# A hybrid encoder layer: the RWKV chunk step as one 128x128 product, low-rank products over padded rows, identities by ScalarE

## The chip, the cores and the metric

The kernel runs on one core of one Trainium2 chip, in one launch. The time is the device time of that launch in microseconds. Before the change it was 1121.99 us, the median of three runs (1121.66 to 1122.10). A change of 1% is 11 us.

## What is computed

One layer of a streaming encoder on x of shape (1, 512, 1024), all in float32:

```
x = x + 1/2 * SwiGLU_1(RMSNorm(x))
p = RMSNorm(x) @ W_in      -> stick-breaking q | k | v  and  RWKV-7 r | k | v | w-lora | a-lora | g-lora
x = x + concat(stick_breaking_attention(q, k, v), rwkv7(...)) @ W_out
x = x + 1/2 * SwiGLU_2(RMSNorm(x))
```

The RWKV half has 8 heads of 64 channels. Its inputs are shifted by one token; two low-rank maps of 64 columns give the decay and the value a:

```
log_w = -softplus(-(w0 + tanh(x_w) @ w2)) - 0.5      # w2: 64 x 512
a     = sigmoid(a0 + x_a @ a2)                       # a2: 64 x 512
S_t = S_{t-1} diag(w_t) + (S_{t-1} a_t) b_t^T + v_t k_t^T ;  y_t = S_t r_t      # for each head
```

followed by a norm for each head, a bonus term and a gate. The state S (64x64 for each head) starts at zero. The kernel computes the recurrence in 8 chunks of 64 tokens: within a chunk the token loop is turned into the inverse of a 64x64 triangular matrix, and from chunk to chunk one product with a 64x64 matrix M carries the state on.

## The kernel before

Activations lie with channels on the 128 partitions and the 512 tokens along the free dimension. Every float32 matrix product of the dense kind is done as three products of rounded halves (`mm3`, L180 to L183: high by high, high by low, low by high), so each weight tile of 128x512 is loaded by SP (`load`), rounded by ScalarE (ACT, L161) and its rest made by VectorE (DVE, L162). A ring of 3 buffers holds each of the raw, high and low tiles.

There are three stages. The first FFN (to about 366 us of the profiled span) makes 22 blocks of the hidden layer and multiplies them by the down weights (`dn`). Blocks 0 to 3 and every third one after them are plain products; the other twelve come in six pairs, each block done by `seven()` with seven products of half size. Of such a block, `pa`, `pc` and `pe` are PSUM banks; `cu` and `h` are tiles of the ring with tag "a" (4 buffers). The finished `h` is split into `hdh` and `hdl`, which go to rings by the list `home` (L398); blocks 2 to 5 go to the ring with tag "r". `parts` (L279) keeps one pair of tiles of that ring until the last block is done.

The middle stage projects, and runs the attention and the RWKV recurrence for four pairs of heads. The low-rank products stand at its start: `lora` (L543) takes w2 from partitions 0 to 63 and a2 from 64 to 127 of one tile `w2a2`, so each of its products uses 64 rows of the TensorE array. For a pair j, `rw_inverse(j)` builds the chunk matrices and `rw_chain(j)` carries the state. Two heads p = 0, 1 lie on partitions 0 to 63 and 64 to 127 (`rows`), and most small products are done for each head apart, with 64 rows and 64 columns of the array. In `rw_inverse`, A is the product of the two halves AR and BK; A's diagonal blocks go through DRAM (`da`), DVE inverts them by 15 substitution steps (L700 to L704, tiles G and H), they come back through DRAM (`db`), and the products `inv` build the inverse from blocks; Z is an identity tile that GpSimd (POOL) fills (`eye`, L508). Then Q, MG and N give the matrix of the chunk step: after L764 the left half of each chunk in AR holds M, with the identity added that POOL wrote at L695. `rw_chain` makes six steps for c = 1 to 6 (L780): two products S = M St, one for each head, then DVE puts PC*S + St into the next chunk's place (L786).

The attention (`att_core`) makes scores z, an Abs, Exp and Ln on ACT, a scan on DVE (l, r), transposes (wT), an Exp (at) and the output o. Its q and k are normalised by `item_qk`, whose result is called rn (L847).

What sets the order: a Python loop at L954 emits pieces of the dense stream and of the three side queues I (inverse), C (chain) and T (attention) by due times; C and I get a priority (L916). The framework's scheduler then orders each engine's instructions by priority and by its own estimate of when operands and buffers come free, and gives each ring buffer to the next tile once its last reader is done. On each engine the order is fixed in the built program, and each engine works it off in turn.

The last stage is the second FFN, built like the first.

Of the kernel before, what the change touches and what calls it, by code (L numbers as in the profile page):

```python
# [16 lines left out]
F32 = mybir.dt.float32  # L17
# [65 lines left out]
def layer(ctx, tc, a, out, dbg=None):  # L83
# [9 lines left out]
        uid[0] += 1  # L93
        return f"{s}_{uid[0]}"

    NB = {"x": 16, "q": 3, "b": 4, "r": 10, "i": 10, "c": 6, "v": 4, "k": 4, "g": 8, "a": 4, "t": 2, "f": 4, "s": 2, "X": 8}
    NM = {"acc": 2, "sd": 1, "mi": 2, "ma": 3}
    NW = 3
    NPL = 4
# [53 lines left out]
    def load(src, n, s="w"):  # L153
        raw = pw.tile([P, T], F32, tag="raw", name=nm(s), bufs=NW)
        nc.sync.dma_start(raw[:, :n], src)
        return raw

    def w_split(raw, n=T, s="w", pool=nc.vector, cp=nc.scalar.copy):
        hi = pw.tile([P, T], F32R, tag="whi", name=nm(s + "h"), bufs=NW)
        lo = pw.tile([P, T], F32R, tag="wlo", name=nm(s + "l"), bufs=NW)  # L160
        cp(hi[:, :n], raw[:, :n])  # L161
        pool.tensor_tensor(lo[:, :n], raw[:, :n], hi[:, :n].bitcast(F32), SUB)  # L162
        return hi, lo

    def load_split(src, n, s="w", pool=None, cp=nc.scalar.copy):
        if pool is None:
            pool = nc.vector
        return w_split(load(src, n, s), n, s, pool, cp)

    mms = []  # L170
    sp = []
# [191 lines left out]
    def ffn(g, wgu, wd, last):  # L363
# [4 lines left out]
        if last:  # L368
            xsrc = pd.tile([KD, P, T], F32, name="xmid")
            for k in range(KD):  # L370
                nc.sync.dma_start(xsrc[k], X[k])
            xs = norm_in(g, XTAG)
            first = None
        else:
            xs = []

            def first():

                ps = [bank(("acc", "ma")[q], "gu"[q]) for q in range(2)]
                z = slot("f", "warm", BF16)  # L380
                nc.vector.memset(z, 0.0)
                for _ in range(11):
                    nc.tensor.matmul(ps[1], lhsT=z[:, 0:P], rhs=z, start=True, stop=True)
                for k in range(KD):
                    if k:
                        nc.sync.dma_start(X[k], a["xT"][k])
                    if k % 4 == 0:
                        w = [load_split(wgu[q][:, k * P:(k + 4) * P], T, pool=nc.vector,
                                        cp=nc.scalar.copy if k or q else nc.vector.tensor_copy) for q in range(2)]
                    xs.append(split(X[k], XTAG[k], v(g, k), "x"))  # L390
                    ks = slice(k % 4 * P, (k % 4 + 1) * P)
                    for q in range(2):
                        mm3(ps[q], w[q][0][:, ks], w[q][1][:, ks], xs[k][0], xs[k][1], k == 0, k == KD - 1)
                nc.sync.dma_start(cst, a["cst"])
                nc.sync.dma_start(lev, a["lev"])
                return ps
# [90 lines left out]
        return  # L487


    w2a2 = slot("g", "w2a2")  # L490
    nc.sync.dma_start(w2a2, a["w2a2"])
    g2 = slot("f", "g2")
    nc.sync.dma_start(g2, a["g2"])
    seg = slot("r", "seg")
# [12 lines left out]

    def eye():  # L508
        z = slot("i", "Z")
        nc.gpsimd.tensor_scalar(c3(z), cs("i64").unsqueeze(1).to_broadcast([P, NCH, CH]), 1.0, None, MUL)  # L510
        return z

    xs = norm_in("nmx")
# [17 lines left out]
    sgx = slot("f", "sgx")  # L531
    act(sgx, xg, AF.Sigmoid)
    Gs, av = [], []
    wh2 = slot("r", "w2h", F32R)
    nc.scalar.copy(wh2, w2a2)
    wl2 = slot("r", "w2l", F32R)
    nc.gpsimd.tensor_tensor(wl2, w2a2, wh2.bitcast(F32), SUB)
    xh2 = slot("r", "xwh", F32R)
    nc.scalar.copy(xh2, xwa)
    xl2 = slot("r", "xwl", F32R)  # L540
    nc.vector.tensor_tensor(xl2, xwa, xh2.bitcast(F32), SUB)

    def lora(ps, js, rs_):  # L543
        mm3(ps, wh2[rs_, js], wl2[rs_, js], xh2[rs_], xl2[rs_], True, True)

    for j in range(4):
        js = slice(j * P, (j + 1) * P)
        pw_ = bank("sd", "lw")
        lora(pw_, js, slice(0, CH))
        sw = slot("r", "sw")  # L550
        act(sw, pw_, AF.Sigmoid, bias=v("w0", j))
        pa_ = bank("sd", "la")
        lora(pa_, js, slice(CH, P))
        aj = slot("g", "a")
        act(aj, pa_, AF.Sigmoid, bias=v("a0", j))
        gj = slot("g", "Gs")
        nc.vector.tensor_tensor_scan(gj, seg, sw, 0.0, MUL, ADD)
        Gs.append(gj)
        av.append(aj)
# [80 lines left out]
    def rw_inverse(j):  # L640
# [37 lines left out]
            nc.scalar.copy(ba[p][:, :, 0:CH], c3(pt[p]))  # L678
        pta = bank("mi", "tA")
        pw0 = bank("mi", "W0")  # L680
        for c in range(NCH):
            cc = slice(c * CH, (c + 1) * CH)
            for p in range(2):
                nc.tensor.matmul(pta[rows[p], cc], lhsT=ar[rows[p], c, 0:CH], rhs=cs("i64")[rows[p]],
                                 start=True, stop=True)
# [3 lines left out]
                o = rows[1 - p]  # L689
                nc.tensor.matmul(pw0[rows[p], cc], lhsT=Aa[p][o, cc], rhs=UV[p][o, cc], start=True, stop=True)  # L690
        At = slot("i", "At")
        nc.scalar.copy(At, pta)
        W0 = slot("i", "W0")
        nc.scalar.copy(W0, pw0)
        nc.gpsimd.tensor_scalar(ar[:, :, 0:CH], cs("i64").unsqueeze(1).to_broadcast([P, NCH, CH]), 1.0, None, MUL)  # L695
        H = slot("i", "H")
        Xb = c3(H[0:NBK, 0:256], SB)
        nc.gpsimd.memset(H[0:NBK, 0:256], 0.0)
# [24 lines left out]
        Xm, XT = X2  # L723


        def prod(l, r):
            ps = bank("mi", "inv")
            for c in range(NCH):
                cc = slice(c * CH, (c + 1) * CH)
                for p in range(2):  # L730
                    l_ = l[p] if isinstance(l, list) else l
                    nc.tensor.matmul(ps[rows[p], cc], lhsT=l_[rows[p], cc], rhs=r[rows[p], cc], start=True, stop=True)
            return ps
# [12 lines left out]
            nc.scalar.copy(XT, pst)  # L746
            yield 6

        pq, pu = prod(XT, At), prod(XT, W0)
        Q = slot("i", "Q")  # L750
        nc.scalar.copy(Q, pq)
        for p in range(2):
            nc.scalar.copy(UV[p][rows[p]], pu[rows[p]])
        yield 3

        for h in range(2):
            hs = slice(4 * h, 4 * h + 4)
            pm = bank("mi", "MG")
            for c in range(4 * h, 4 * h + 4):
                cp = slice((c % 4) * P, (c % 4 + 1) * P)  # L760
                for p in range(2):
                    nc.tensor.matmul(pm[rows[p], cp], lhsT=Q[rows[p], c * CH:(c + 1) * CH], rhs=ba[p][rows[p], c],
                                     start=True, stop=True)
            nc.vector.tensor_tensor(ar[:, hs], c3(pm, P), ar[:, hs], ADD)  # L764
        pn = bank("mi", "N")
        for c in range(NCH - 1):
            cc = slice(c * CH, (c + 1) * CH)
            for p in range(2):
# [1 line left out]
        St = slot("i", "St")  # L770
        nc.vector.tensor_tensor(c3(St)[:, 1:NCH], c3(pn)[:, 0:NCH - 1],
                                PC[:, 0:NCH - 1].unsqueeze(2).to_broadcast([P, NCH - 1, CH]), MUL)
        ctxs[j].update(ba=ba, ar=ar, St=St)
        yield 3

    def rw_chain(j):

        js = slice(j * P, (j + 1) * P)
        PC, ar, ba, bv, UV, St = (ctxs[j][n] for n in ("PC", "ar", "ba", "bv", "UV", "St"))
        for c in range(1, NCH - 1):  # L780
            cc = slice(c * CH, (c + 1) * CH)
            nn = slice((c + 1) * CH, (c + 2) * CH)
            pS = bank("mi", "S", [P, CH])
            for p in range(2):
                nc.tensor.matmul(pS[rows[p]], lhsT=ar[rows[p], c, 0:CH], rhs=St[rows[p], cc], start=True, stop=True)
            nc.vector.scalar_tensor_tensor(St[:, nn], pS, PC[:, c:c + 1], St[:, nn], MUL, ADD)  # L786
            yield 1.2

        py = bank("mi", "y")
        for c in range(NCH):  # L790
            cc = slice(c * CH, (c + 1) * CH)
            for p in range(2):
                nc.tensor.matmul(py[rows[p], cc], lhsT=UV[p][:, cc], rhs=ba[p][:, c, CH:P], start=c == 0, stop=False)
        for c in range(1, NCH):
            cc = slice(c * CH, (c + 1) * CH)
            for p in range(2):
                nc.tensor.matmul(py[rows[p], cc], lhsT=St[rows[p], cc], rhs=ar[rows[p], c, CH:P],
                                 start=False, stop=c == NCH - 1)

        yc = slot("r", "yc")  # L800
        nc.scalar.copy(yc, py)
        yr = slot("r", "yr")
        act(yr, py, AF.Square)
        pv = bank("mi", "var")
        head_sum(pv, yr)
        act(yr, pv, AF.Ln, scale=1.0 / CH, bias=epsl)
        act(yr, yr, AF.Exp, scale=-0.5)
        nc.vector.scalar_tensor_tensor(yr, yc, v("lnw", j), yr, MUL, MUL)
        nc.vector.scalar_tensor_tensor(yr, yr, v("lnb", j), bv, ADD, ADD)
        pg = bank("mi", "g")  # L810
        nc.tensor.matmul(pg, lhsT=g2[:, js], rhs=sgx, start=True, stop=True)
        o = slot("g", "orw")
        nc.vector.tensor_tensor(o, pg, yr, MUL)
        outs[4 + j] = o
        yield 5
# [174 lines left out]
def host_arrays(inp):  # L990
# [24 lines left out]

    w = i["w_out"].reshape(2, 4, P, 4, 2, P)[::-1]
    d["wo"] = np.ascontiguousarray(w.transpose(1, 3, 2, 4, 0, 5)).reshape(16, P, T)
    d["w2a2"] = np.ascontiguousarray(np.concatenate([i["rw_w2"], i["rw_a2"]], 0))
    d["g2"] = np.ascontiguousarray(i["rw_g2"])
    return d  # L1020

# [18 lines left out]
```

## Time and profile before

| | before |
|---|---|
| median of 3 runs | 1121.99 us |
| profiled execution | 1122.11 us, span 1120.3 us |
| granted TensorE clock, mean | 0.995 |
| TensorE products (PE) busy | 1090.7 us, 97% |
| VectorE (DVE) busy | 727.5 us, 65% |
| ScalarE (ACT) busy | 520.6 us, 46% |
| GpSimd (POOL) busy | 79.3 us, 7% |
| chain that ended last, by engine | PE 78%, DVE 13%, ACT 3% |

The span is the time from the first to the last instruction; the profiled execution took 1.8 us more than its span. A row for a product gives the rows and columns of the array as 128*128, 64*128 (64 rows) or 64*64, then the partitions and elements that move. Float32 products run as two passes, and each pass is a row of its own in the counts; rounded halves (fp32r) run as one. The ends of products are modelled, so the text compares starts. A clock of 1.00 is 2.4 GHz, and the lower level is 1.2 GHz.

### The profile page before, as it was taken

Reading aid. Unit: us, or ns where it says so; the run is one execution under the profiler, and the core shown is the slowest. Engines: PE = TensorE matmul, PEld = TensorE weight load, DVE = VectorE, ACT = ScalarE, POOL = GpSimd, SP = SyncE. Lnnn points to the kernel's source line nnn. Section 1 sums busy time; section 2 is a strip of 40 time slices with the busy share of each in tenths; the row PEclk is TensorE's granted clock in tenths of the full one; section 3 lists DMA queues with packets and bytes.
Section 4 is the critical chain, followed back from the end, with each engine's and each line's share of the span. In section 5 each row is a group of like instructions: output and inputs, shape, how many; then the busy total and the mean of one; then the engine's idle time right before and its main releaser. Section 6 shows DMA issues by size and latency. Waiting matters only on the chain.

```text
span 1120.3 us, 18878 instructions
## 1 busy us (share of the span) xinstructions
PE 1090.7 (97%) x7363; PEld 896.7 (80%) x7363; DVE 727.5 (65%) x1296; ACT 520.6 (46%) x958; POOL 79.3 (7%) x61
## 2 busy tenths in 40 slices
PE   8989999999999999999999998998999999999998
PEld 6789999998888767766667675676889999998886
DVE  6997777763333567577766768587987777753322
ACT  5555545543223564474644554454555545432221
POOL 0100000000003011011100310012100000000000
PEclk9999999999999999999999999999999999999999
DMA  5333333343333224311211211043343333344442
GB/s 193 107 106 95 112 104 114 96 138 101 95 98 94 95 66 140 81 38 50 58 31 50 48 32 39 20 132 124 93 122 101 98 90 109 95 146 113 115 120 62
DMA packets 70697, 104.23 MB, mean 93 GB/s; under 512 B 19664, under 2 KB 21840, under 8 KB 70608
## 3 DMA queue, kind: packets, MB, share of 16 engines
q1 hardware_dynamic: 70608, 103.02, 31.1%
q8 instruction: 58, 0.95, 0.3%
q14 instruction: 31, 0.25, 0.1%
HBM read 97.23 MB, written 5.77 MB: 92 GB/s over the span
## 4 chain that ended last, share of the span: by engine, by line
PE 78%; DVE 13%; ACT 3%; issue 2%; POOL 1%; DMA 1%; SPq 0%; DVEq 0%; ACTq 0%; POOLq 0%
PE dn L183 7%; PE dn L182 7%; PE dn L181 7%; PE pa L181 4%; PE pa L183 4%; PE pa L182 4%; PE g L182 2%; PE g L181 2%; PE g L183 2%; PE pc L183 2%; PE pc L182 2%; PE pc L181 2%; PE u L181 2%; PE u L183 2%; PE u L182 2%
## 5 line engine op out<-in xcount | busy, mean ns | idle before, releaser
L162 DVE TENSOR_TENSOR wl<-w,wh 128x512 fp32r<-128x512 f32 x220 | 151.0, 687 | 200.6 <-ACT wh L161 199.4
L161 ACT CAST wh<-w 128x512 fp32r<-128x512 f32 (+1 forms) x219 | 132.2, 604 | 237.7 <-PE dn L182 153.6
L181 PE MATMUL dn<-hdh,wh 128*128 128x512 f32 x240 | 93.4, 389 | 0.0
L182 PE MATMUL dn<-hdl,wh 128*128 128x512 f32 x240 | 93.4, 389 | 0.0
L183 PE MATMUL dn<-hdh,wl 128*128 128x512 f32 x240 | 93.4, 389 | 0.0
L182 PEld LDWEIGHTS dn<-hdl,wh 128*128 128x128 f32 x240 | 45.1, 188 | 9.3
L181 PEld LDWEIGHTS dn<-hdh,wh 128*128 128x128 f32 x240 | 45.1, 188 | 9.3
L183 PEld LDWEIGHTS dn<-hdh,wl 128*128 128x128 f32 x240 | 45.1, 188 | 9.3
L161 ACT CAST wh<-wg 128x512 fp32r<-128x512 f32 x48 | 29.7, 621 | 38.2 <-PE u L182 21.0
L181 PE MATMUL dn<-hd,wh 128*128 128x512 f32 x112 | 43.6, 389 | 0.0
L182 PE MATMUL dn<-hd,wh 128*128 128x512 f32 x112 | 43.6, 389 | 0.0
L183 PE MATMUL dn<-hd,wl 128*128 128x512 f32 x112 | 43.6, 389 | 0.0
L183 PE MATMUL u<-xnh,wl 128*128 128x512 f32 x96 | 37.5, 390 | 0.9 <-DVE wl L162 0.9
L181 PE MATMUL g<-xnh,wh 128*128 128x512 f32 x96 | 37.6, 391 | 0.0
L182 PE MATMUL g<-xnl,wh 128*128 128x512 f32 x96 | 37.5, 391 | 0.0
L182 PE MATMUL u<-xnl,wh 128*128 128x512 f32 x96 | 37.5, 390 | 0.0
L181 PE MATMUL u<-xnh,wh 128*128 128x512 f32 x96 | 37.5, 390 | 0.0
L183 PE MATMUL g<-xnh,wl 128*128 128x512 f32 x96 | 37.5, 390 | 0.0
L162 DVE TENSOR_TENSOR wl<-wg,wh 128x512 fp32r<-128x512 f32 x48 | 33.0, 686 | 5.5 <-ACT wh L161 5.5
L315 ACT CAST s3h<-s 128x512 fp32r<-128x512 f32 x24 | 14.9, 621 | 41.3 <-DVE s L313 41.3
L181 PE MATMUL pa<-xch,s2h 128*128 128x256 f32 x96 | 27.4, 285 | 3.5 <-ACT cu L332 3.5
L134 ACT ACTIVATE l<-l 128x128 f32<-128x128 f32 (+3 forms) x64 | 28.8, 467 | 0.9
(355 smaller groups left out, 3197.3 us busy)
## 6 DMA issues: line engine op xcount, KB each, us to landing
w<-wgu SPq DMA_DIRECT2D x80, 256.0 KB, 2.9
w<-wd SPq DMA_DIRECT2D x80, 256.0 KB, 2.6
wu<-wgu SPq DMA_DIRECT2D x48, 256.0 KB, 2.9
wg<-wgu SPq DMA_DIRECT2D x48, 256.0 KB, 2.5
w<-wrw SPq DMA_DIRECT2D x28, 256.0 KB, 2.8
x<-xT SPq DMA_DIRECT2D x16, 256.0 KB, 4.8
w<-wqk SPq DMA_DIRECT2D x16, 256.0 KB, 2.7
wv<-wv SPq DMA_DIRECT2D x16, 256.0 KB, 2.6
```

Source lines behind the costliest of these rows:

```text
L134: ins = nc.scalar.activation(out_, in_, func, **kw)
L161: cp(hi[:, :n], raw[:, :n])
L162: pool.tensor_tensor(lo[:, :n], raw[:, :n], hi[:, :n].bitcast(F32), SUB)
L181: mms.append(nc.tensor.matmul(ps, lhsT=lh, rhs=rh, start=start, stop=False, skip_group_check=again))
L182: nc.tensor.matmul(ps, lhsT=lh, rhs=rl, start=False, stop=False, skip_group_check=again)
L183: nc.tensor.matmul(ps, lhsT=ll, rhs=rh, start=False, stop=stop, skip_group_check=again)
L315: nc.scalar.copy(hi, t_)
```

## The change

Four things change.

The chunk step: a new tile `Mb` (ring "m", one buffer) holds for each chunk a 128x128 matrix with head 0's M in the upper left block, head 1's in the lower right, and zero elsewhere. POOL sets it to zero, DVE writes the two blocks from the bank MG with the identity added, and the step is one product with 128 rows and columns. AR keeps only its right half, so POOL's identity in its left half goes, and DVE's addition for AR covers 64 of 128 columns of each chunk. Chunk 0 (whose state before is zero) is left out of tA, of the product with At and of MG.

The low-rank products: `w2a2` becomes two tiles, w2 with zeros below and a2 with zeros above, and each product takes all 128 rows. They need two more tiles of ring "r" and one more load.

Identities: `eye` copies with ACT.

Rings: "r" has 8 buffers instead of 10, which makes room for `Mb`.

```
-    NB = {"x": 16, "q": 3, "b": 4, "r": 10, "i": 10, "c": 6, "v": 4, "k": 4, "g": 8, "a": 4, "t": 2, "f": 4, "s": 2, "X": 8}
+    NB = {"x": 16, "q": 3, "b": 4, "r": 8, "i": 10, "c": 6, "v": 4, "k": 4, "g": 8, "a": 4, "t": 2, "f": 4, "s": 2, "X": 8, "m": 1}
...
-    w2a2 = slot("g", "w2a2")
-    nc.sync.dma_start(w2a2, a["w2a2"])
+    w2a2 = [slot("g", "w2a2") for _ in range(2)]
+    for q in range(2):
+        nc.sync.dma_start(w2a2[q], a["w2a2"][q])
...
     def eye():
         z = slot("i", "Z")
-        nc.gpsimd.tensor_scalar(c3(z), cs("i64").unsqueeze(1).to_broadcast([P, NCH, CH]), 1.0, None, MUL)
+        nc.scalar.copy(c3(z), cs("i64").unsqueeze(1).to_broadcast([P, NCH, CH]))
...
-    def lora(ps, js, rs_):
-        mm3(ps, wh2[rs_, js], wl2[rs_, js], xh2[rs_], xl2[rs_], True, True)
+    def lora(ps, js, q):
+        mm3(ps, w2[q][0][:, js], w2[q][1][:, js], xh2, xl2, True, True)
...
-        for c in range(NCH):
+        for c in range(1, NCH):
...
-        nc.gpsimd.tensor_scalar(ar[:, :, 0:CH], cs("i64").unsqueeze(1).to_broadcast([P, NCH, CH]), 1.0, None, MUL)
+        Mb = quad("Mb", tag="m")
+        mb = c3(Mb, P)
+        nc.gpsimd.memset(Mb, 0.0)
...
-        pq, pu = prod(XT, At), prod(XT, W0)
+        pq, pu = prod(XT, At, 1), prod(XT, W0)
...
         for h in range(2):
-            hs = slice(4 * h, 4 * h + 4)
+            c0 = max(4 * h, 1)
+            hs = slice(c0, 4 * h + 4)
             pm = bank("mi", "MG")
-            for c in range(4 * h, 4 * h + 4):
+            for c in range(c0, 4 * h + 4):
...
-            nc.vector.tensor_tensor(ar[:, hs], c3(pm, P), ar[:, hs], ADD)
+            n = 3
+            for p in range(2):
+                nc.vector.tensor_tensor(mb[rows[p], c0:c0 + n, p * CH:(p + 1) * CH],
+                                        c3(pm, P)[rows[p], c0 % 4:c0 % 4 + n, 0:CH],
+                                        cs("i64")[rows[p]].unsqueeze(1).to_broadcast([CH, n, CH]), ADD)
+            nc.vector.tensor_tensor(ar[:, hs, CH:P], c3(pm, P)[:, c0 % 4:, CH:P], ar[:, hs, CH:P], ADD)
...
-            for p in range(2):
-                nc.tensor.matmul(pS[rows[p]], lhsT=ar[rows[p], c, 0:CH], rhs=St[rows[p], cc], start=True, stop=True)
+            nc.tensor.matmul(pS, lhsT=mb[:, c], rhs=St[:, cc], start=True, stop=True)
```

The host array w2a2 becomes (2, 128, 512) with the zeros in it.

The order of the instructions changes with it, since buffers and products differ. Three places follow. A row names the line, the operation, and its tiles with their buffer numbers; x2 stands for two instructions in a row.

On PE, in the chunk steps of the first pair, before:

```order
L785 MATMUL S_5514<-St_5263,AR_4252 64x64 x2
L183 MATMUL k_5096<-xh_3718,wl_5100 128x512
L181 MATMUL k_5096<-xh_3722,wh_5099 128x512
L182 MATMUL k_5096<-xl_3723,wh_5099 128x512
L785 MATMUL S_5536<-St_5263,AR_4252 64x64 x2
```

and after:

```order
L795 MATMUL S_5517<-St_5268,Mb_4513 128x64
L180 MATMUL k_5101<-xl_3737,wh_5122 128x512
L181 MATMUL k_5101<-xh_3736,wl_5123 128x512
L179 MATMUL k_5101<-xh_3740,wh_5122 128x512
L795 MATMUL S_5538<-St_5268,Mb_4513 128x64
```

Each step is one product over all 128 rows instead of two over 64; the dense products between two steps are as many.

On DVE, at the last pair of heads, the end of the substitution (G and H), with the normalised q and k (rn, of qc) of the last attention item between its steps, before:

```order
L704 TENSOR_REDUCE H_7194<-G_7112 64x12
L809 SCALAR_TENSOR_TENSOR yr_7275<-yr_7275,vec,xv_5304 128x512
L702 TENSOR_TENSOR G_7112<-G_7112,H_7194 64x169
L813 TENSOR_TENSOR orw_7285<-g_7283,yr_7275 128x512
L704 TENSOR_REDUCE H_7194<-G_7112 64x13
L847 SCALAR_TENSOR_TENSOR rn_6298<-qc_6296,derived,rn_6298 128x512
L702 TENSOR_TENSOR G_7112<-G_7112,H_7194 64x196
L847 SCALAR_TENSOR_TENSOR rn_6347<-qc_6345,vec,rn_6347 128x512
```

and after, with the beginning of the same substitution:

```order
L854 TENSOR_TENSOR rn_6345<-qm_6347,S_3829 128x512
L923 TENSOR_TENSOR x_2852<-wo_6808,x_2852 128x512
L857 SCALAR_TENSOR_TENSOR rn_6345<-qc_6343,vec,rn_6345 128x512
L796 SCALAR_TENSOR_TENSOR St_7064<-S_7223,PC_5607,St_7064 128x64
L706 TENSOR_TENSOR G_7102<-G_7102,H_7179 64x1
L708 TENSOR_REDUCE H_7179<-G_7102 64x1
L706 TENSOR_TENSOR G_7102<-G_7102,H_7179 64x4
```

The rn of q and of k have moved from the end of the substitution to a place ahead of its first step.

On ACT, in the first FFN, at a pair of blocks (h_1079 is the older block's result, h_1164 and cu_1163 the newer one's tiles), before:

```order
L134 ACTIVATE cu_1078<-cu_1078 128x512
L337 COPY h_1164<-pc_1161 128x256
L315 CAST s4h_1320<-s_301_1318 128x512
L161 CAST wh_1360<-w_1358 128x512
L193 CAST hd_1258<-h_1079 128x512
L342 COPY cu_1163<-pa_1160 128x256
```

and after:

```order
L134 ACTIVATE cu_1078<-cu_1078 128x512
L313 CAST s4h_1320<-s_301_1318 128x512
L161 CAST wh_1360<-w_1358 128x512
L335 COPY h_1164<-pc_1161 128x256
L191 CAST hd_1258<-h_1079 128x512
L340 COPY cu_1163<-pa_1160 128x256
```

The copy of `pc` has moved behind two casts, and in the built program it now waits for DVE, which must have read the older block's tiles; the split of block 5's result has moved from its place to the end of the block loop.

## Rows read from the trace of the kernel before

**Rows 1.** The page: PE's busy time, and the chain by engine.
```profile
PE 1090.7 (97%) x7363; PEld 896.7 (80%) x7363; DVE 727.5 (65%) x1296; ACT 520.6 (46%) x958; POOL 79.3 (7%) x61
PE 78%; DVE 13%; ACT 3%; issue 2%; POOL 1%; DMA 1%; SPq 0%; DVEq 0%; ACTq 0%; POOLq 0%
```

**Rows 2.** Stages: stretch, length, busy PE PEld DVE ACT POOL, clock, DMA, GB/s.
```profile
380.00:405.00 25.00, 25.00 (x93) 15.76 (x92) 13.29 (x16) 16.88 (x26) 1.35 (x1) 1.00 0.17 53
...
600.00:700.00 100.00, 92.79 (x887) 64.08 (x887) 80.62 (x179) 54.99 (x115) 14.92 (x10) 0.98 0.18 44
```

**Rows 3.** PE in order of time at a chunk step: start, us, instruction.
```profile
515.85 0.40 PE L182 MATMUL k<-xl,wh 128*128 128x512 f32 x1
516.18 0.33 PE L785 MATMUL S<-St,AR 64*64 64x64 f32 x4
516.44 0.50 PE L183 MATMUL k<-xh,wl 128*128 128x512 f32 x1
516.78 0.39 PE L181 MATMUL k<-xh,wh 128*128 128x512 f32 x1
517.01 0.40 PE L182 MATMUL k<-xl,wh 128*128 128x512 f32 x1
```

**Rows 4.** PE in order of time at a low-rank product.
```profile
387.50 0.40 PE L182 MATMUL k<-xl,wh 128*128 128x512 f32 x1
387.83 0.49 PE L181 MATMUL la<-xwh,w2h 64*128 64x512 f32 x1
...
389.06 0.40 PE L181 MATMUL k<-xh,wh 128*128 128x512 f32 x1
```

**Rows 5.** PE in order of time at the norm's sum over partitions.
```profile
371.38 0.39 PE L183 MATMUL wa<-xh,wl 128*128 128x512 f32 x1
371.61 0.95 PE L219 MATMUL ms<-ones,sq 128*128 128x1 f32 x8
372.42 0.49 PE L181 MATMUL xg<-xh,wh 128*128 128x512 f32 x1
```

**Rows 6.** The chain in order of time, 440 to 800: start, us, what.
```profile
463.19 3.26 PE inv L732 x96
...
471.94 1.09 PE MG L762 x16
```

**Rows 7.** Groups by line, 440 to 800: count, busy us, mean ns, idle before.
```profile
L764 DVE TENSOR_TENSOR AR<-MG,AR 128x512 f32<-128x512 f32 x8 | 5.5, 689 | 22.9 <-PE MG L762 22.9
L658 DVE TENSOR_TENSOR Aa<-A,cst 128x256 f32<-128x256 f32 x12 | 4.9, 412 | 2.5 <-PE A L655 2.5
L746 ACT COPY XT<-inv 128x512 f32<-128x512 f32 x8 | 4.7, 586 | 12.1 <-PE inv L732 11.5 <-issue 0.6
```

**Rows 8.** Waits of PE's weight loads, 440 to 800: us, times, longest.
```profile
PEld MG L762 <- DVE AR L764: 1.3, 3, 0.8
```

**Rows 9.** The page's DMA issues: count, KB each, us to landing.
```profile
w<-wrw SPq DMA_DIRECT2D x28, 256.0 KB, 2.8
```

**Rows 10.** PE in order of time at its longest wait, with that wait in brackets.
```profile
678.60 0.49 PE L857 MATMUL z<-rn,rn 64*128 64x128 f32 x4 [3.28 <-DVE rn L847]
...
680.05 0.63 PE L183 MATMUL wo<-orh,wol 128*128 128x512 f32 x1
680.48 0.63 PE L181 MATMUL wo<-osh,woh 128*128 128x512 f32 x1
...
683.47 0.39 PE L181 MATMUL wo<-osh,woh 128*128 128x512 f32 x1
```

**Rows 11.** DVE in order of time before that wait ends.
```profile
677.80 0.75 DVE L847 SCALAR_TENSOR_TENSOR rn<-qc,vec,rn 128x512 f32<-128x512 f32 x1
```

**Rows 12.** DVE, ACT and PE in order of time at a pair of blocks.
```profile
115.14 0.42 DVE L360 TENSOR_TENSOR h<-pa,cu 128x256 f32<-128x256 f32 x1 [0.45 <-PE pa L183]
...
116.58 0.37 ACT L342 COPY cu<-pa 128x256 f32<-128x256 f32 x1 [0.19 <-PE pa L183]
...
117.82 0.28 PE L181 MATMUL pa<-xch,s3h 128*128 128x256 f32 x1
```

More of the change, by code (lines that the diff above doesn't have):

```diff
@@ L156, in load, with w_split @@
         return raw
-    def w_split(raw, n=T, s="w", pool=nc.vector, cp=nc.scalar.copy):
+    def w_split(raw, n=T, s="w", cp=nc.scalar.copy):
         hi = pw.tile([P, T], F32R, tag="whi", name=nm(s + "h"), bufs=NW)
@@ L161, in w_split, with load_split @@
         cp(hi[:, :n], raw[:, :n])
-        pool.tensor_tensor(lo[:, :n], raw[:, :n], hi[:, :n].bitcast(F32), SUB)
+        nc.vector.tensor_tensor(lo[:, :n], raw[:, :n], hi[:, :n].bitcast(F32), SUB)
         return hi, lo
[L165 to L168, printed above, removed]
+    def load_split(src, n, s="w", cp=nc.scalar.copy):
+        return w_split(load(src, n, s), n, s, cp)
     mms = []
@@ L387, in first @@
                     if k % 4 == 0:
-                        w = [load_split(wgu[q][:, k * P:(k + 4) * P], T, pool=nc.vector,
+                        w = [load_split(wgu[q][:, k * P:(k + 4) * P], T,
                                         cp=nc.scalar.copy if k or q else nc.vector.tensor_copy) for q in range(2)]
@@ L533, in layer @@
     Gs, av = [], []
[L534 to L537, printed above, removed]
+    w2 = []
+    for q in range(2):
+        wh2, wl2 = slot("r", "w2h", F32R), slot("r", "w2l", F32R)
+        nc.scalar.copy(wh2, w2a2[q])
+        nc.gpsimd.tensor_tensor(wl2, w2a2[q], wh2.bitcast(F32), SUB)
+        w2.append((wh2, wl2))
     xh2 = slot("r", "xwh", F32R)
@@ L548, in layer @@
         pw_ = bank("sd", "lw")
-        lora(pw_, js, slice(0, CH))
+        lora(pw_, js, 0)
         sw = slot("r", "sw")
@@ L552, in layer @@
         pa_ = bank("sd", "la")
-        lora(pa_, js, slice(CH, P))
+        lora(pa_, js, 1)
         aj = slot("g", "a")
@@ L691, in rw_inverse @@
         At = slot("i", "At")
-        nc.scalar.copy(At, pta)
+        nc.scalar.copy(At[:, CH:], pta[:, CH:])
         W0 = slot("i", "W0")
         nc.scalar.copy(W0, pw0)
-        nc.gpsimd.tensor_scalar(ar[:, :, 0:CH], cs("i64").unsqueeze(1).to_broadcast([P, NCH, CH]), 1.0, None, MUL)
+        Mb = quad("Mb", tag="m")
+        mb = c3(Mb, P)
+        nc.gpsimd.memset(Mb, 0.0)
         H = slot("i", "H")
@@ L723, in rw_inverse, with prod @@
         Xm, XT = X2
-        def prod(l, r):
+        def prod(l, r, c0=0):
             ps = bank("mi", "inv")
-            for c in range(NCH):
+            for c in range(c0, NCH):
                 cc = slice(c * CH, (c + 1) * CH)
@@ L747, in rw_inverse @@
             yield 6
-        pq, pu = prod(XT, At), prod(XT, W0)
+        pq, pu = prod(XT, At, 1), prod(XT, W0)
         Q = slot("i", "Q")
-        nc.scalar.copy(Q, pq)
+        nc.scalar.copy(Q[:, CH:], pq[:, CH:])
         for p in range(2):
@@ L772, in rw_inverse @@
                                 PC[:, 0:NCH - 1].unsqueeze(2).to_broadcast([P, NCH - 1, CH]), MUL)
-        ctxs[j].update(ba=ba, ar=ar, St=St)
+        ctxs[j].update(ba=ba, ar=ar, mb=mb, St=St)
         yield 3
@@ L778, in rw_chain @@
         js = slice(j * P, (j + 1) * P)
-        PC, ar, ba, bv, UV, St = (ctxs[j][n] for n in ("PC", "ar", "ba", "bv", "UV", "St"))
+        PC, ar, mb, ba, bv, UV, St = (ctxs[j][n] for n in ("PC", "ar", "mb", "ba", "bv", "UV", "St"))
         for c in range(1, NCH - 1):
@@ L1017, in host_arrays @@
     d["wo"] = np.ascontiguousarray(w.transpose(1, 3, 2, 4, 0, 5)).reshape(16, P, T)
-    d["w2a2"] = np.ascontiguousarray(np.concatenate([i["rw_w2"], i["rw_a2"]], 0))
+    d["w2a2"] = np.zeros((2, P, T), np.float32)
+    d["w2a2"][0, :CH] = i["rw_w2"]
+    d["w2a2"][1, CH:] = i["rw_a2"]
     d["g2"] = np.ascontiguousarray(i["rw_g2"])
```

## The prediction

> **What bounds the kernel now.** I read the page's busy times and chain first: PE is busy for 97% of the span and carries 78% of the chain that ended last [rows 1]. Then the stage table: through the low-rank products PE has no idle time at all, and in the attention and RWKV stage, at its worst stretch, it still works 92.8 of 100 us, with DVE at 80.6 and ACT at 55 [rows 2]. So a microsecond taken out of PE's stream there is a microsecond of the kernel, unless a wait opens. Then I read PE's instructions in order of time, around the products that change.
>
> In a dense run one 128x512 product starts 0.23 us after the last (516.78 to 517.01). With a chunk step between, 515.85 to 516.78 is 0.93 us where two dense intervals are 0.46: the step costs 0.47 us, though its four passes of 64x64 are tiny [rows 3]. The low-rank product shows why. Its three products of 64 rows cost as much in time as dense ones, yet 387.50 to 389.06 holds five intervals, 1.15 us, and lasts 1.56 [rows 4]. The 0.41 us too many lie at the two places where the array changes from 128 rows to 64 and back; the first shows in the 0.33 from 387.50 to 387.83. That is 0.21 us per change of shape, and for the chunk step 0.41 of its 0.47.
>
> **The change, part by part.** I go through PE's two listings and give each product the rows and columns of the array it uses. Before, the shape changes 241 times, now 179 times. Of the 62 that go, 18 belong to the low-rank products (nine visits, the first being broken in two); the rest are the chunk steps, less what the new order adds elsewhere. At 0.21 that is -13.0 us.
>
> The step itself: its passes now cost 0.47 - 0.41 = 0.06, 24 times 1.4 us. Afterwards a step is two passes with 128 columns of weights and 64 moving columns. No such product is in the trace. The nearest is the norm's sum over partitions, also f32 with 128x128 weights and one moving column: eight passes between two dense products take 371.61 to 372.42, 0.81 us, 0.10 each [rows 5]. From below it is the 0.034 of a 64x64 pass in an unbroken run (3.26 us for 96) [rows 6]; from above a dense product's 0.23. I take 0.10, the row nearest in shape: 0.20 a step, 24 steps 4.8, so +3.4 us net (from 0.2 to 9.6).
>
> Chunk 0 is left out of three sets. In tA and in the product with At, 4 passes of 0.034, 0.14 us, twice for each of four head pairs: -1.1. In MG, 4 passes of 1.09/16 = 0.07, four times: -1.1 [rows 6]. PE in all: -13.0 + 3.4 - 2.2 = -11.8 us, on the path because PE is.
>
> DVE: two 128x512 additions of 0.69 for each pair become six instructions, five of 192 columns and one of 256. A 256-column one takes 0.41 [rows 7]; between the two sizes the slope is 0.0011 us a column, so 192 columns take 0.34 (0.31 if it went by columns alone, 0.41 at most). A pair: 5 x 0.34 + 0.41 = 2.11 against 1.38, four pairs +2.9 us (2.3 to 4.3). Queued behind them are St, whose product starts the chunk chain, and the bank of MG that N wants. Each bank is now held for three instructions, 1.0 us instead of 0.7. Today PE waited for that bank three times, 1.3 us [rows 8]. I put all eight banks at 0.3 on the path: +2.4, out of 0 to 4.3.
>
> The identities: eight copies on ACT at 0.59 [rows 7], 4.7 us, beside PE's work on an engine that is busy for 55 of 100 us; none hangs on data of the step, so I cost them at nothing, 4.7 if that cover is gone. POOL is rid of eight Z and four AR fills and gets a memset of Mb, with H's memset queued behind it; DVE's substitution waits for H, PE does not. The second half of w2a2 is one more 256 KB load on SP (2.8 us to landing [rows 9]), past which the weights of the next products are issued, and one more cast and subtraction; they lie in the stretch where the DMA engines are busy for 17% [rows 2]. Nothing, or up to 2.8.
>
> The order: the scheduler has moved whole items. PE now waits 3.28 us at 675 for the last pair's normalised q and k, and for 3.4 us behind that wait the clock is at its lower level (dense starts 0.43 apart, 680.05 to 680.48): up to 683.47 seven dense products and one transpose take 3.42 us instead of 7 x 0.23 + 0.1 = 1.7 [rows 10]. Cause: DVE makes the last rn at 677.80 only, between the substitution's steps [rows 11]. In the new order both rn stand ahead of that substitution. So -3.3 - 1.7 = -5.0 (from 0, if another such wait comes, to -5.0); I take -4.5, since DVE and ACT have more to do elsewhere.
>
> Sum against the profiled execution's own 1122.11 us (span 1120.3 and 1.8 around it, 0.1 over the median of 1121.99): 1122.1 - 11.8 + 2.4 - 4.5 = 1108.2. **I forecast 1108.2 us.**
>
> A rule that speaks against this: the Trainium skill, TensorEngine Tiling (Array Packing), Theoretical Speedup, has up to 2x for each dimension of 64 or less by splitting the array, so that joining two 64x64 products would give a gain away. By that rule alone the step would only get dearer; the same page (Key Properties) also says that a change of tiling mode drains the engine, and by that the trace agrees with its 0.21 us. The first result is rival 3.
>
> **The rivals.**
> 1. *DVE takes a part back.* For it: 80.6 of 100 us busy, and the stall at 675 was DVE's. If the stall stays in some other place and all 2.9 us of new DVE work end on the path: 1122.1 - 11.8 + 2.9 = 1113.2. Against: the waits of PE for DVE are short elsewhere.
> 2. *All of it comes.* The banks are never waited for and the stall goes whole: 1122.1 - 11.8 - 5.0 = 1105.3.
> 3. *The gaps do not come from the shape but from any small f32 product.* Then no change of shape is won, the step costs 24 x (0.20 - 0.14) = 1.4 more, the fewer products give 2.2, the stall goes: 1122.1 + 1.4 - 2.2 + 2.4 - 4.5 = 1119.2. Against: the low-rank product is not f32-slow and has the gap; the norm's passes are f32 and have none.
> 4. *Slower: the shorter ring.* Ring r has 8 buffers instead of 10, and in both FFNs the hidden tile of block 5 must wait for the end of the block loop to be split, holding one of the four buffers of ring a. So "h<-pc" on ACT now stands behind the old block's last product, with "cu<-pa" two behind it, and PE needs that bank for s3. Place: five pairs in each FFN. Price: today the old product ends on DVE at 115.14 + 0.42, the copy of cu starts at 116.58 and takes 0.37, PE comes at 117.82: 0.87 us of room [rows 12]. The copy in front costs 0.37, so it decides only from half a microsecond of further lateness; 1.9 us too late each would give 1108.2 + 10 x 1.9 = 1127. Against: the cast that stood between has moved ahead of it.
>
> **How the numbers follow.** Forecast 0.55, its own range 1104 to 1112; rival 1 0.17, rival 2 0.13, rival 3 0.06, rival 4 0.07, something else 0.02. The range of 8 in 10 takes in rivals 1 and 2 and the dear end of the step's price (+6.2 over the forecast, 1114) and stops short of 3 and 4: 1102 to 1118. A difference of 0.2% (2.2 us) is about what a measurement here can tell from none. Faster 0.89, the same 0.04 (part of rival 3), slower 0.07.
>
> **What will show it.** Right: between two dense products a chunk step costs 0.2 us instead of 0.47; the low-rank products run at 0.23 with no 0.33 beside them; PE's idle time in the stage does not grow; no 3 us wait and no slow clock near 675. Wrong: steps that still cost 0.4 (rival 3); "issue" time before PE replaced by waits for Mb, St or Z (rival 1); in the FFNs, waits of "pa" for "cu" (rival 4), which would make the time miss by most.

## The result, and the profile after

The changed kernel takes 1109.99 us (median; 1109.11 to 1110.19) where the kernel before took 1122.1 in the same session: a ratio of 0.9887, 95% interval 0.9873 to 0.9902, or 12.1 us less. The forecast was 1108.2 with a range of 1102 to 1118. The time came out 1.8 us from the forecast; the places where it comes from are only partly those that the forecast named.

The profiled execution of the changed kernel took 1110.0 us, its span is 1108.2. Its page answers to [rows 1]; the two stretches and the whole middle stage answer to [rows 2] (stretch, length, busy PE PEld DVE ACT POOL, clock, DMA, GB/s):

```profile
PE 1084.6 (98%) x7267; PEld 898.1 (81%) x7267; DVE 734.8 (66%) x1312; ACT 521.1 (47%) x967; POOL 63.0 (6%) x54
PE 83%; DVE 10%; ACT 3%; issue 2%; DMA 1%; POOL 0%; SPq 0%; DVEq 0%; POOLq 0%; ACTq 0%
```
```profile
372.09:745.65 373.56, 364.26 (x3171) 266.64 (x3170) 277.09 (x553) 204.14 (x391) 29.92 (x30) 0.99 0.22 62
380.00:405.00 25.00, 25.00 (x101) 17.99 (x101) 14.74 (x19) 17.97 (x28) 2.64 (x2) 1.00 0.21 64
600.00:700.00 100.00, 95.52 (x902) 65.67 (x902) 80.27 (x168) 56.07 (x121) 4.68 (x6) 0.97 0.18 43
672.80:679.20 6.40, 6.40 (x17) 4.33 (x17) 4.38 (x12) 2.10 (x6) 0.00 (x0) 0.50 0.00 0
```

The middle stage, from the first product of xg to the first product of the second feed-forward stage, took 384.13 us in the kernel before:

```profile
372.42:756.55 384.13, 371.12 (x3266) 265.71 (x3266) 271.65 (x537) 201.58 (x382) 47.08 (x38) 1.00 0.22 61
```

So 10.6 of the 12.1 us lie in this stage. The rest (0.3 before it, 1.2 behind it) lies in code that is the same in both, but for the order of some instructions; in the experiments below, the time up to the stage varies by -1.7 to +3.1 us, the time from there to the last product by -0.85 to +0.5, whatever the kernel. From here on the stage alone is compared between profiles.

I split its time in three. *Waits* are the bracketed waits in PE's rows in order of time (20 before, 16 after). *Slow clock* is an estimate of what PE loses while the granted clock is 0.50: half of that stretch, since dense starts are 0.43 apart there and 0.23 elsewhere (672.80 to 679.20 above and 0.4 us at its edges make 3.4; before, 1.7). What is left is PE's *own work*. Before: 12.1 + 1.7 + 370.3. After: 8.3 + 3.4 + 361.9. So the own work fell by 8.5 us, waits and slow clock together by 2.1.

The chunk step between two dense products, against [rows 3]:

```profile
513.33 0.39 PE L181 MATMUL k<-xh,wl 128*128 128x512 f32 x1
513.55 0.33 PE L795 MATMUL S<-St,Mb 128*128 128x64 f32 x2
513.69 0.48 PE L179 MATMUL k<-xh,wh 128*128 128x512 f32 x1
514.01 0.39 PE L180 MATMUL k<-xl,wh 128*128 128x512 f32 x1
```

513.33 to 514.01 is 0.68 us, less two dense intervals of 0.23: the step costs 0.22, where 0.20 was forecast, and 0.47 before. It is made of other parts than forecast: the two passes take 0.14 us to the next product's start, not 0.20, and the dense product behind them takes 0.32 instead of 0.23, a gap at full shape for which the forecast had nothing. And three of the 24 steps now stand inside the run of W, a run of 64x64 products. There two 64x64 products had been nearly free, 0.01 us from their start to the next product's, first in the kernel before:

```profile
522.59 0.27 PE L785 MATMUL S<-St,AR 64*64 64x64 f32 x2 [0.27 <-ACT At L692]
522.60 0.27 PE L690 MATMUL W<-UV,Aa 64*64 64x64 f32 x2
522.70 0.23 PE L785 MATMUL S<-St,AR 64*64 64x64 f32 x2
522.71 0.46 PE L690 MATMUL W<-UV,Aa 64*64 64x64 f32 x10
```

and after:

```profile
521.06 0.43 PE L795 MATMUL S<-St,Mb 128*128 128x64 f32 x2
521.43 0.56 PE L692 MATMUL W<-UV,Aa 64*64 64x64 f32 x10
```

There the step takes 0.37 us (521.06 to 521.43). A low-rank product; first the three rows of the kernel before that [rows 4] leaves out, then the changed kernel:

```profile
388.16 0.39 PE L182 MATMUL la<-xwl,w2h 64*128 64x512 f32 x1
388.39 0.39 PE L183 MATMUL la<-xwh,w2l 64*128 64x512 f32 x1
388.72 0.50 PE L183 MATMUL k<-xh,wl 128*128 128x512 f32 x1
```

```profile
387.68 0.39 PE L181 MATMUL k<-xh,wl 128*128 128x512 f32 x1
387.93 0.50 PE L179 MATMUL la<-xwh,w2h 128*128 128x512 f32 x1
388.27 0.39 PE L180 MATMUL la<-xwl,w2h 128*128 128x512 f32 x1
388.50 0.40 PE L181 MATMUL la<-xwh,w2l 128*128 128x512 f32 x1
388.73 0.39 PE L179 MATMUL k<-xh,wh 128*128 128x512 f32 x1
```

Before, four starts were 0.33 or 0.34 apart instead of 0.23 (387.50, 387.83, 388.39 and 388.72 to the next); three of these four gaps are gone, and the first product still takes 0.34. A visit, the three products together, costs 0.13 us above dense work, where it was 0.41. And the place of the stall of [rows 10]:

```profile
669.37 0.40 PE L181 MATMUL wo<-osh,wol 128*128 128x512 f32 x1
671.57 0.33 PE L886 MATMUL wT<-cst,r 128*128 128x128 f32 x1 [1.80 <-DVE r L879]
...
676.37 0.63 PE L179 MATMUL wo<-osh,woh 128*128 128x512 f32 x1
676.80 0.63 PE L180 MATMUL wo<-osl,woh 128*128 128x512 f32 x1
...
679.36 0.41 PE L180 MATMUL wo<-osl,woh 128*128 128x512 f32 x1
```

The wait for rn is gone. A wait of 1.80 us for r, attention's weights of the same head pair, stands nearly in its place, and the clock behind it is low for twice as long: dense starts 0.43 apart up to 679.36. The two together cost 5.2 us where the old pair cost 5.0.

### The profile page after: what moved, and what is told of

It is laid out like the page before. It is cut to its first block, busy times and chain, and to the rows that moved or that the text cites. A ratio compares the mean times of both kernels' runs of the same rounds, so it can differ in the third digit from the quotient of the medians.

```text
span 1108.2 us, 18729 instructions
## 1 busy us (share of the span) xinstructions
PE 1084.6 (98%) x7267; PEld 898.1 (81%) x7267; DVE 734.8 (66%) x1312; ACT 521.1 (47%) x967; POOL 63.0 (6%) x54
## 4 chain that ended last, share of the span: by engine, by line
PE 83%; DVE 10%; ACT 3%; issue 2%; DMA 1%; POOL 0%; SPq 0%; DVEq 0%; POOLq 0%; ACTq 0%
PE dn L179 7%; PE dn L180 7%; PE dn L181 7%; PE pa L179 4%; PE pa L181 4%; PE pa L180 4%; PE g L180 3%; PE g L181 3%; PE g L179 3%; PE u L181 2%; PE u L179 2%; PE u L180 2%; PE inv L736 2%; PE pc L181 2%; PE pc L180 2%; PE pc L179 2%
```

## The experiments

All were timed against the kernel before. The first two columns are of the timed runs, the others of each profile's middle stage, worked out as above ("changes" are the changes of array shape in PE's listing, the fixed order of its instructions).

| kernel | median us | ratio, 95% interval | stage | waits | slow clock | own work | changes |
|---|---|---|---|---|---|---|---|
| before | 1122.1 | 1 | 384.1 | 12.1 | 1.7 | 370.3 | 241 |
| after | 1110.0 | 0.9887 (0.9873-0.9902) | 373.6 | 8.3 | 3.4 | 361.9 | 179 |
| step_alone | 1122.5 | 1.0002 (0.9992-1.0012) | 385.4 | 14.2 | 5.1 | 366.1 | 203 |
| lowrank_alone | 1119.5 | 0.9976 (0.9965-0.9987) | 382.4 | 13.0 | 3.4 | 365.9 | 220 |
| eye_alone | 1118.9 | 0.9972 (0.9958-0.9986) | 380.1 | 9.9 | 0 | 370.2 | 239 |
| before_ring8 | 1119.6 | 0.9973 (0.9963-0.9984) | 382.2 | 11.3 | 0 | 370.9 | 239 |
| after_two64 | 1113.1 | 0.9921 (0.9899-0.9943) | 377.6 | 8.8 | 3.4 | 365.4 | 211 |
| after_chunk0 | 1114.4 | 0.9928 (0.9912-0.9943) | 378.6 | 11.4 | 3.4 | 363.8 | 182 |
| after_eye_pool | 1116.2 | 0.9940 (0.9924-0.9956) | 378.1 | 11.9 | 5.1 | 361.1 | 178 |
| after_relu_act | 1110.8 | 0.9894 (0.9875-0.9912) | 375.0 | 10.3 | 3.4 | 361.3 | 180 |
| after_pool_reads | 1109.4 | 0.9893 (0.9873-0.9912) | 373.6 | 8.4 | 3.4 | 361.8 | 179 |
| after_pool_writes | 1109.1 | 0.9892 (0.9872-0.9912) | 373.5 | 8.1 | 3.4 | 362.0 | 179 |
| after_slow_att | 1109.2 | 0.9886 (0.9867-0.9906) | 372.0 | 10.6 | 0 | 361.4 | 175 |
| after_slower_att | 1110.6 | 0.9897 (0.9877-0.9916) | 375.3 | 11.1 | 3.4 | 360.8 | 182 |

The column of own work says how far it can be trusted: the kernels with before's products lie between 370.2 and 370.9, the seven with the changed kernel's products between 360.8 and 362.0. Where a wait lies inside the low-clock stretch, half of it is counted twice, and own work comes out too small by as much: 0.9 us in after_eye_pool, 0.4 in after_chunk0.

**The step alone.** Undone against the changed kernel: the low-rank products, the identities, and chunk 0's absence from tA, the product with At and MG.

> The chunk step alone, in the kernel before: Mb, one 128x128 product, MG's addition in six instructions, ring r of 8; the low-rank products stay at 64 rows, the identities on GpSimd, and chunk 0 is computed in tA, the product with At and MG. Its PE listing has 203 changes of shape, 38 fewer than before. Forecast theory (0.21 us a change, a step of 0.20 us): 38 x 0.21 = -8.0, +3.4 for the passes, +2.4 for MG's banks: 1119.9 if the stall at 675 stays, 1115.4 if it goes (both rn stand earlier in the listing, one of them still inside the substitution). Rival 3 (a gap for any small f32 product): +1.4 + 2.4 and no gain: 1126 with the stall, 1121.4 without.

Own work fell by 4.3 us; 38 x 0.21 less 3.4 had been -4.6, and rival 3 wanted +1.4. That part is right. But the time is the same as before, nearer to rival 3's second sum than to either of the forecast's, because waits and slow clock grew by 5.6 us. The largest group (us, times, longest):

```profile
PE wT L882 <- DVE r L875: 8.3, 11, 2.2
```

Eleven waits of attention's transposes for r, where the kernel before had six of 2.9 us in all. Both sums of the expectation missed this.

**The low-rank products alone.**

```
-    def lora(ps, js, rs_):
-        mm3(ps, wh2[rs_, js], wl2[rs_, js], xh2[rs_], xl2[rs_], True, True)
+    def lora(ps, js, q):
+        mm3(ps, w2[q][0][:, js], w2[q][1][:, js], xh2, xl2, True, True)
```

> The low-rank products over padded rows alone, in the kernel before; nothing else changes, the listing keeps its order and has 21 changes of shape fewer. Forecast theory: 21 x 0.21 = -4.4, so 1117.7, with the stall at 675 as before; a low-rank visit shows no 0.33 beside it. From what the changed kernel's trace shows (some 0.13 us a visit left over), -2.5, so 1119.6. Rival 3: the same time as before, 1122, with the 0.41 us of a visit still there.

1119.5 is the second number. The visits show the same 0.13 as in the changed kernel, nine of them 9 x 0.28 = 2.5 us; own work fell by 4.4, of which these rows explain 2.5. Rival 3, by which the 0.41 would have stayed, falls here too.

**The identities alone.**

```
-        nc.gpsimd.tensor_scalar(c3(z), cs("i64")..., 1.0, None, MUL)
+        nc.scalar.copy(c3(z), cs("i64")...)
```

> The identities by ScalarE alone, in the kernel before. Forecast theory: nothing hangs on the eight copies, 1122 within 1 us, as long as the stall at 675 stays (in the listing one rn moves ahead, the other stays behind the substitution); if the stall goes, 1117.6. Rival: the copies lie on ACT's path to PE, 4.7 us more, 1126.8, with waits of PE for Z or for tiles that ACT makes.

1118.9 lies near the second number, the stall gone. Own work is unchanged (370.2), no wait for rn is left, and no slow clock. What is left for Z, against 2.0 us and four waits before, and a new wait of wo (us, times, longest):

```profile
PE wo L181 <- DVE x L913: 2.7, 1, 2.7
...
PE inv L732 <- DVE Z L738: 0.6, 2, 0.4
```

**The step as two 64x64 products again, in the changed kernel.**

```
-            nc.tensor.matmul(pS, lhsT=mb[:, c], rhs=St[:, cc], ...)
+            for p in range(2):
+                nc.tensor.matmul(pS[rows[p]], lhsT=mb[rows[p], c, p*CH:(p+1)*CH],
+                                 rhs=St[rows[p], cc], ...)
```

> The changed kernel with one thing undone: the step is again two 64x64 products, taken from the two blocks of Mb; Mb, its zeros, MG's six additions, the low-rank products, chunk 0 and the identities stay. The listing has 32 changes of shape more than the changed kernel. Forecast theory: +32 x 0.21 = 6.7, less 24 x 0.14 = 3.4 for the dearer passes that go: 1113.3, and a step between dense products costs 0.47 again. Rival 3 (the gap comes from any small f32 product): the step costs what it costs now or less, 1110 or below (1106.6 if only the passes get cheaper).

1113.1, and own work +3.5 us: the forecast's numbers. The operand and the sums are the same; the shape differs, and with it the number of passes, four for two:

```profile
516.76 0.40 PE L181 MATMUL k<-xh,wl 128*128 128x512 f32 x1
517.08 0.33 PE L796 MATMUL S<-St,Mb 64*64 64x64 f32 x4
517.35 0.50 PE L179 MATMUL k<-xh,wh 128*128 128x512 f32 x1
517.68 0.40 PE L180 MATMUL k<-xl,wh 128*128 128x512 f32 x1
```

0.92 us from 516.76 to 517.68, 0.46 without the two dense intervals. Rival 3, by which no change of shape is won, is refuted: the step loses half of its price at 128x128. That it is two passes instead of four doesn't explain it, since inside the run of W the four take 0.02 us.

**Identities by GpSimd in the changed kernel** (the edit of eye_alone, reversed).

> The changed kernel with the identities made by GpSimd again. The listing has 178 changes of shape (the changed kernel 179), so TensorE's own work should be the same; both rn of the last pair stand before or one of them inside its substitution (808 and 819 against 812 to 851). What the run of the identities alone showed (3.5 us won, and DVE's instruction with two SBUF inputs, X<-G,cst, at 0.68 us instead of 0.81 us beside the fill) says that the fills on GpSimd slow DVE and that PE's waits grow: 2 to 5 us more than the changed kernel, 1112 to 1115, X<-G,cst at 0.81 again. The prediction's own reading (nothing hangs on the place of the eight fills): 1110 within 1 us.

5.9 us slower by the ratios (0.9940 against 0.9887), in the stage 4.5: own work is the same, waits and slow clock grew by 5.3. The clock is at 0.50 for ten microseconds:

```profile
372.48:750.57 378.09, 365.18 (x3170) 267.26 (x3170) 279.12 (x553) 201.41 (x383) 42.91 (x38) 0.99 0.22 62
671.00:681.00 10.00, 8.64 (x22) 5.30 (x23) 7.00 (x17) 3.72 (x10) 0.00 (x0) 0.50 0.28 52
```

The time, 1116.2, is just above the first theory's 1112 to 1115. Its sign is not there: X<-G,cst takes 0.82 us in the changed kernel too, which has no fill on GpSimd, and the mean comes from one slow instruction of eight (last section). But VectorE is busy 2.0 us longer for the same 553 instructions, 279.1 against 277.1. The longest waits are for r, 2.2 and 1.4 us near 671 and 673; none is for Z.

**Chunk 0 computed again** (`range(NCH)` in tA, the product with At and MG, whole copies).

> The changed kernel with chunk 0 computed again in tA, the product with At and MG (24 more small products in all). Forecast theory: +2.2 us of TensorE's time, apart from what the order does: both rn of the last pair stand behind the start of its substitution in this listing (817 and 830 against 810), so a wait like the one at 675 of the kernel before may come back, up to 5 more. With the wait 1117, without it 1112. Rival: the small products of chunk 0 cost next to nothing (0.03 us each in a run), 1111 without the wait. The stage time less its waits and less what the slow clock costs tells the two apart.

Own work +1.9 (forecast 2.2, the rival 0.8); waits and slow clock +3.1. The wait that the expectation feared is small, 0.2 us for rn; two waits of wT for r, 2.1 and 1.4 us, stand at 671 and 673. The time lies between the two sums, 1112 and 1117.

**Ring r alone.** `"r": 10` to `"r": 8` in the kernel before.

> The kernel before with ring r at 8 buffers instead of 10 and nothing else. Forecast theory: no wait of pa for cu beyond the 3.4 us that are there, 1122 within 2 us, whatever the order makes of the middle stage. Rival 4 (the shorter ring makes cu late in both feed-forward stages): up to 10 to 19 us in these stages.

Rival 4 is refuted: pa's waits for cu are 3.5 us, as before and in the changed kernel. An edit that saves no work made the kernel 2.6 us faster, by another listing in the middle stage: waits and slow clock 2.5 less.

**VectorE relieved.** `nc.vector.tensor_scalar(r, pz, 0.0, None, MAX)` becomes ScalarE's Relu.

> The changed kernel with one more edit: the positive part of the scores (r<-z, 32 instructions, some 15 us of VectorE's time by their sizes) is taken by ScalarE as Relu instead of by VectorE. Theory: what is left of PE's waits in the middle stage is VectorE being late (wT waits for r 3.8 us in all, and behind the longest, 1.8 us, the clock is low for 6.8 us, which costs 3.4): with VectorE relieved 3 to 6 us of the changed kernel's time go, 1104 to 1107. Rival: the waits belong to the order of the listing or to the chain z, l, r, wT itself, which gets longer on ScalarE: 1110 or above.

VectorE's busy time in the stage fell from 277.1 to 263.5 us and the waits grew by 2.0:

```profile
372.46:747.49 375.03, 363.41 (x3170) 266.39 (x3170) 263.51 (x521) 212.39 (x423) 30.03 (x30) 0.99 0.22 62
```

So relieving VectorE doesn't shorten these waits. The rival's time came; which of its two causes it is, the listing or the longer chain on ScalarE, this run doesn't tell.

**GpSimd reads, GpSimd writes.** Two kernels with the changed kernel's listing, four copies from X or three memsets on GpSimd behind each `eye()`:

```
+            for q in range(4):
+                nc.gpsimd.tensor_scalar(dm, Xm[:, q * P:(q + 1) * P], 1.0, None, MUL)
```

> The changed kernel, identities still by ScalarE, with four extra GpSimd copies of 128x128 from the inverse's X tile into a scratch tile at each of the eight places where GpSimd filled an identity before (they leave the result alone); the listings of TensorE, VectorE and ScalarE keep the changed kernel's order but for one product moved by four rows. Theory A (GpSimd instructions that read SBUF slow VectorE's with two SBUF inputs, and that is what the identities cost on GpSimd): X<-G,cst rises from 0.68 us towards 0.8, VectorE is busy 2 us longer in the middle stage, and the whole run is 3 to 6 us slower, 1113 to 1116. Theory B (what the place of the identities cost is the lateness of Z itself and the listing that came with it): 1110 within 1.5 us, even if X<-G,cst rises.

> The same with a tiny copy (128x4, to wait for X) and three GpSimd memsets of 128x128 in place of the four copies: GpSimd works at the same places but hardly reads SBUF; the listings keep the same order. Theory A and theory B: 1110 within 1.5 us, X<-G,cst stays at 0.68.

Both take the changed kernel's time. The copies kept GpSimd busy for 21.2 us more, more than the eight identities had (14.0):

```profile
370.97:744.58 373.61, 364.15 (x3170) 266.62 (x3170) 277.49 (x553) 203.84 (x391) 50.66 (x62) 0.99 0.22 62
L745 POOL TENSOR_SCALAR dm<-X 128x128 f32<-128x128 f32 x32 | 21.2, 662 | 118.9 <-DVE X L725 94.5 <-ACT X L751 22.3
```

A GpSimd that is busy there costs nothing by itself. Theory A is not tested by this, though: it wanted VectorE busy for 2 us longer, and beside the copies, which wait for X and so start behind VectorE's instruction, it is busy for 0.4 longer (277.5 against 277.1). With the fills it was busy longer: by 2.0 us in after_eye_pool, and by 2.6 in the kernel before against eye_alone (271.7 and 269.1). Whether that reaches the time stays open. X<-G,cst stayed at 0.82 in both (the expected 0.68 was wrong). With the same listing, stage, waits and slow clock come back within 0.2 us: they belong to the listing, not to chance.

**Attention spread wider.** `"T": 0.7` to 0.9 and 1.1 in the scheduler's table.

> The changed kernel with one number of the scheduler changed: attention's steps count 0.9 a unit instead of 0.7, so they are spread wider among the dense products; 175 changes of shape instead of 179, no arithmetic changed. Theory (the waits of wT for r and the slow clock behind them, 11.7 us of the middle stage in the changed kernel, belong to the listing alone): the sum of the two moves by some us either way with TensorE's own work at about 361.9 us as now; my guess is a gain, 1106 to 1110. Rival (they belong to VectorE's load): 1110 within 1 us.

> The same with 1.1 a unit: 182 changes of shape, and in the listing six waits of wT stand close behind their scores instead of ten. By the same theory 1104 to 1112, with TensorE's own work of the middle stage at 362; by the rival 1110 within 1 us.

With 0.9 no slow clock is left, but waits are 2.3 longer; with 1.1 the waits are 2.8 longer. Own work stays. Neither time can be told from the changed kernel's, so no version here beats it; the times fit theory and rival alike, and only the split speaks for the theory.

## Why the prediction was right, point by point

- *Low-rank products* (18 x 0.21 = -3.8): direction and cause right, the size too large. Of the 0.41 at a visit 0.13 is not shape: the first product has its extra 0.10 at full shape too. The rows give -2.5; the kernel alone -4.4 in own work, of which 1.9 has no row that I can point to. A gap at full shape stood in the trace before, too: the dense product behind the norm's passes, 372.42 in [rows 5], is followed only 0.32 later, so that "the norm's passes are f32 and have none" was misread.

```profile
372.74 0.40 PE L182 MATMUL xg<-xl,wh 128*128 128x512 f32 x1
```

- *Chunk steps* (the other 44 changes, -9.2, and +3.4 for the passes: -5.8): -4.3 alone, -3.5 as the last edit. The 0.22 was forecast within 0.02, in part by luck: passes 0.06 cheaper, and a gap of 0.09 behind them that was left out. Wrong was to pay every change in the listing 0.21. Place by place against after_two64, the ten of the 24 steps between two dense products win about 0.24, five beside the f32 products om and qm, also 128x128, win 0.13 to 0.24, three in the run of W lose 0.35 to 0.6 each, and next to tB or A a step wins about 0.1 or nothing. This is the term that failed most.
- *Chunk 0* (-2.2): -1.9.
- PE in all: -8.5 instead of -11.8.
- *MG on VectorE* (2.11 us a pair, +2.9): 16 x 0.353 + 8 x 0.391 = 8.8 us, +3.3 against 5.5. On the path I put +2.4; PE waited for that bank 0.2 us, once. The waits of [rows 8] were those of weight loads, and no row of PE's products had one.

```profile
L772 DVE TENSOR_TENSOR Mb<-MG,cst 64x192 f32<-64x192 f32 x16 | 5.6, 353 | 8.7 <-PE MG L768 8.6
L775 DVE TENSOR_TENSOR AR<-MG,AR 128x192 f32<-128x192 f32 (+1 forms) x8 | 3.1, 391 | 0.1
```

- *Identities* (nothing): in PE's own work nothing, as forecast; in waits and slow clock enough to move the time by 3.5 us alone and by 5.9 in the changed kernel. How much of that is another listing, and how much the fills themselves (with them Z is later and VectorE 2.0 to 2.6 us busier), the runs don't separate. I had put this gain under "order" and tied it to no edit.
- *The order* (-4.5 at 675): wrong as told. The wait for rn went, and a wait for r with a longer low clock cost as much (5.2 against 5.0). What the stage gained in waits came from elsewhere: 2.0 us for Z gone, rn's 3.3 gone, wT's grown from 2.9 to 3.8, slow clock +1.7; with the small ones -2.1. The forecast's two terms, +2.4 and -4.5, also make -2.1, by luck.
- *Rivals.* 3 is refuted by after_two64, 4 by before_ring8. 2 was right that the banks are hardly waited for and wrong that the stall goes whole. 1 named the right danger (the stall comes back in another place) with a cause that isn't borne out: in after_relu_act less work on VectorE doesn't remove it.

So in the stage I forecast -13.9 and got -10.6; 1.5 us fell outside it, where the forecast had nothing and no edit is known to save any. That the total is off by only 1.8 us is luck to that extent. What decides how long the waits of one listing are is not settled: the runs show only that equal listings repeat them and that small edits move their sum with the slow clock between 9.9 and 19.4 us.

## What to carry to other kernels

Count shape changes of the array where they happen: joining two 64x64 products into one 128x128 with zeros pays between full-shape products and loses inside a run of 64x64 ones. Where a scheduler reorders everything at any edit, compare TensorE's work without its waits and slow clock, or an edit that does nothing will look like a gain of 2.6 us (ring r) and one that saves 4 us like none (the step alone). Beside the edit's price, predict a spread for the listing.

## What the runs showed of the hardware that I had not expected

- The length of a low-clock stretch doesn't follow the wait ahead of it: 3.28 us of wait had 3.4 us at 0.50 behind it before, 1.80 us had 6.8 after, with small products first and ten dense ones behind. In all fourteen stages the clock cost 0, 1.7, 3.4 or 5.1 us.
- Two f32 passes with 128x128 weights and 64 columns take 0.14 us from their start to the next product's (513.55 to 513.69), four of 64x64 took 0.26 [rows 3].
- VectorE's X<-G,cst takes 0.67 us, but the second of one pair in the changed kernel takes about 1.7 (2.38 for the two), beside a GpSimd product of two SBUF tiles that started before this second one:

```profile
617.49 2.38 DVE L723 TENSOR_TENSOR X<-G,cst 128x512 f32<-128x512 f32 x2
617.65 1.68 POOL L623 TENSOR_TENSOR BK<-kkn,Pi 64x512 f32<-64x512 f32 x1 [0.63 <-DVE kkn L619]
```

In the kernel before, a fill of Z that had started first makes VectorE's wl take 1.05 us instead of 0.68:

```profile
460.80 1.93 POOL L510 TENSOR_SCALAR Z<-cst 128x512 f32<-128x512 f32 x1 [25.81 <-DMA w<-wrw]
461.34 1.05 DVE L162 TENSOR_TENSOR wl<-w,wh 128x512 fp32r<-128x512 f32 x1
```

Where VectorE starts first, GpSimd pays. In the first pair of after_pool_reads X<-G,cst stays at 0.64 each, and the copy that starts beside it takes 0.90 us, where the median copy takes 531 ns (ns: shortest, median, longest). In eye_alone GpSimd's BK, begun behind VectorE's, takes 5.40 us beside VectorE instructions that keep their times, X<-G,cst at 0.67 among them:

```profile
457.69 1.28 DVE L725 TENSOR_TENSOR X<-G,cst 128x512 f32<-128x512 f32 x2
458.47 0.90 POOL L745 TENSOR_SCALAR dm<-X 128x128 f32<-128x128 f32 x1 [38.33 <-DVE X L725]
L745 POOL TENSOR_SCALAR dm<-X x32: 528/531/1152, 458.5 to 700.4; 128x128 f32<-128x128 f32 x32
```
```profile
627.65 0.67 DVE L621 TENSOR_TENSOR BK<-kf,Pi 64x512 f32<-64x512 f32 x1
627.81 5.40 POOL L621 TENSOR_TENSOR BK<-kkn,Pi 64x512 f32<-64x512 f32 x1 [0.63 <-DVE kkn L617]
629.46 0.67 DVE L719 TENSOR_TENSOR X<-G,cst 128x512 f32<-128x512 f32 x1
```

The Trainium skill, SBUF — State Buffer, Who interferes with whom, has it that a VectorE instruction with two SBUF inputs contends with a GpSimd instruction that reads SBUF. All four places agree: in each, the one that started later took longer.
